# A table in place of the planner for the order of every engine, other buffer counts, and 256 more rows of x that come transposed from the host

## The chip, the cores and the metric

The kernel runs on one core of one Trainium2 chip. The metric is the device time of one execution in microseconds (us); shorter is better. A core has five engines with an instruction stream each: PE (TensorE, matrix products), DVE (VectorE), ACT (ScalarE), POOL (GpSimd) and SP (SyncE, which here only issues DMAs). Each runs its own stream strictly in order and waits for others on semaphores.

## What is computed

One layer over 2048 tokens of 1024 channels, batch 1, all in float32:

```
proj = rmsnorm(x) @ w_in                 # 1024 -> 3072: u, gate_ssm, q, k, v, gate_attn, 512 each
y_ssm = S5(u): complex diagonal scan over time (32 groups, 64 states), GELU, GLU
y_att = stick-breaking attention(q, k, v): 8 heads of 64, strictly causal, q and k RMS-normed
h = x + concat(y_ssm * silu(gate_ssm), y_att * silu(gate_attn)) @ w_out
out = h + sigmoid(rmsnorm(h) @ w_ple_gate) * (p @ w_ple_proj)
```

## The kernel before, in words

The 2048 tokens are 16 blocks of 128, taken two at a time (a pair T = 0 to 7 has 256 tokens). Each float32 operand of a large product is split into a high part, rounded to a narrower type that PE takes, and the rest: ACT writes the high part and DVE the low one (`split`, L511 to L514; for weights `load_w`, L473 to L496). A product is then three matmuls: high by high, high by low, low by high (`mm3`, L536, and `mm3x`, L702).

The work goes through four stages. First `phase_u` (L546): u for all eight pairs, 96 matmuls of 128x256 for each pair (8 chunks of the 1024 channels, 4 column tiles, 3 products). Meanwhile DVE works through `ssm_chain`, some hundreds of short operations that prepare the scan. Second, from L1204, the gate of the SSM half for every pair (`gate_unit`, L642) together with the eight batches of the scan (`ssm_pack`, `ssm_batch`) and the first attention projections. Third, from L1228, 40 steps of attention in four passes of two heads each, one pass 8 steps behind the other: `attn_proj` (L712) makes q, k, v and the gate of a block two blocks ahead, `attn_block` (L795) does one block of queries, and late steps carry the GLU (`glu_unit`) and sums of weights. Fourth, `phase_out` (L1038): the output projection and the gated embedding, each with a scheme of seven half-size products in place of eight.

**Where the rows of x come from.** The products need x transposed (channels on partitions), and scaled by its norm. For pair 0 (`load_plain`, L552) the host hands over the first 256 rows of x already transposed (`turned_x`, L1610). They are split as they are, without the norm; the norm of each token is worked out beside the products (`norms`, L573: squares on ACT, three adds on POOL, a sum by PE against ones, a power on POOL, and a product with a diagonal that spreads it into `e.row`), and multiplied in where the products leave PSUM: L633 for u, L656 for the gate, L735 and L748 for attention. For pairs 1 to 7 (`load_x`, L588) the plain rows are loaded by DMA (L593), squared and summed on ACT (L596), normed through DVE and POOL (L597, `rms_rstd`), scaled on ACT (L598), transposed by PE in 16 pieces of 64x64 for each block (L526), and split. Both forms then write the split block to DRAM (`hn_d`), from which later stages read it. The plain rows rest in XB = 4 buffers of one block each.

**PSUM.** u's four column tiles of a pair take one bank each: for pair 0 from the list w0, w1, o, acc, z0, z1, for later pairs from w0, w1, o, acc, in turn (L620). The transposes of `load_x` go through z0 and z1. So pair 1 takes the four banks that pair 0 filled.

**One block of attention** (L805 to L844) walks over up to four chunks of 512 keys, the newest first. For each chunk: products of q and k into `ps_z` (contraction over the 64 channels of a head, two heads abreast on the two halves of PE's rows), a sigmoid on ACT (L816), a running product on DVE (L821), 64x64 transposes on PE into `ps_wt`, and a copy with 1 - x on ACT into `ws` (L835). The products of `ws` with v into `ps_o` (L843; 64 output columns, two heads abreast on the two halves of PE's columns) are not made chunk by chunk but held until HOLD = 2 chunks have gathered or the block ends. A block with one or two chunks thus has one such burst, a block with three or four has two. `ws` rests in WSB = 5 buffers.

**The order.** The program is first written down in the order of the Python code. `arrange` (L1563) then gives every engine its order: `plan` works out for each instruction which others it needs and, by `duration` (L1295), an estimated length; `best_order` (L1530) runs a list scheduler forward and backward six times and keeps the order with the shortest estimated end. Two hints matter at the start: what is written inside `e.first()` ranks ahead of all else, and DMAs inside `e.later(k)` start no sooner than the instruction marked k (mark 0 is the load of weight chunk 7, L484). The order is fixed when the program is built; on the chip nothing is reordered.

The 16 KB at the start of each SBUF partition is scratch for the descriptors of DMAs that POOL issues: 8 writes of u (L638), the table of the scan, some constants, and the loads of the first pair of `phase_out`.

## Time and profile before

| what | before |
|---|---|
| median of 3 runs (lowest to highest) | 1474.67 us (1472.99 to 1477.0) |
| the profiled execution | 1474.24 us |
| its span, first to last instruction | 1472.5 us |
| mean granted clock of TensorE | 0.994 |
| busy: PE, weight loads beside it, DVE, ACT, POOL | 98%, 83%, 69%, 55%, 32% |
| instructions | 33586 |

The profile is of one execution, whose time is 1.7 us over its span (start and end lie around it) and 0.4 us under the median. In its lines an engine's name is followed by the line of the kernel, the operation, the tile written, an arrow and the tiles read. In a timeline the first two columns are the start and the length in us, and a bracket names the idle time before and what ended it. A matmul's length is the time until its result is out; matmuls overlap, so the pace is read from one start to the next. In the stage table (a window per row) each engine has its busy time and, in parentheses, its instructions.

### The profile page before, as it was taken

The page shows a single profiled execution, that of the slowest core. Times are in us where ns is not written, and L with a number is a line of the kernel's source. Part 1 is how long each engine was busy: PE and PEld are TensorE (multiplying, and loading weights), DVE is VectorE, ACT ScalarE, POOL GpSimd, SP SyncE. Part 2 cuts the span into 40 slices and gives each one's busy share as a digit, 9 for nine tenths or more (in the row PEclk, how much of TensorE's full clock was granted, in tenths as well). Part 3 has the DMA queues.
Part 4 walks back from the last instruction along what each step waited for, and adds up shares of the span by engine and source line. Part 5 has one row for each costly group of instructions (what it writes and reads, how often), then busy time and mean ns, then how long its engine had stood idle before and what let it go on. Part 6 is the DMA issues. An engine that isn't in the chain of part 4 may idle for free.

```text
span 1472.5 us, 33586 instructions
## 1 busy us (share of the span) xinstructions
PE 1436.7 (98%) x13068; PEld 1224.2 (83%) x13068; DVE 1009.0 (69%) x1817; ACT 810.4 (55%) x1765; POOL 474.8 (32%) x512
## 2 busy tenths in 40 slices
PE   6999999999999999999999999999999999999998
PEld 5999889988888888888888877777778888778786
DVE  8953977977567786678766775666778557754444
ACT  5654555565555766567655665555665345533432
POOL 3131363522221211221121124443334554534432
PEclk8999999999999999999999999999999999999999
DMA  8886845645333433334332455766568556523221
GB/s 289 288 287 205 250 143 186 206 143 168 128 130 125 144 112 114 114 130 140 121 126 102 142 146 171 226 218 178 155 201 280 176 171 200 166 65 101 93 72 58
DMA packets 179054, 238.21 MB, mean 162 GB/s; under 512 B 65760, under 2 KB 121296, under 8 KB 167760
## 3 DMA queue, kind: packets, MB, share of 16 engines
q1 hardware_dynamic: 176512, 227.49, 48.0%
q0 software_dynamic: 2384, 8.59, 2.0%
q8 instruction: 103, 1.69, 0.5%
q14 instruction: 55, 0.45, 0.1%
HBM read 166.94 MB, written 64.90 MB: 157 GB/s over the span
## 4 chain that ended last, share of the span: by engine, by line
PE 81%; DVE 7%; DMA 3%; ACT 3%; issue 3%; POOL 2%; SPq 1%; POOLq 0%; DVEq 0%; ACTq 0%
PE ps_q L745 21%; PE ps_o L843 7%; PE ps_z L812 6%; PE ps_wt L526 4%; PE ps_g L707 4%; PE ps_h L709 4%; PE ps_h L707 3%; PE ps_h L708 3%; PE ps_g L709 3%; PE ps_g L708 3%; DMA v<-qn 2%; PE ps_u L541 1%; PE ps_u L543 1%; PE ps_u L542 1%; PE ps_sg L541 1%
## 5 line engine op out<-in xcount | busy, mean ns | idle before, releaser
L821 DVE TENSOR_TENSOR_SCAN px<-px,ps_z 128x512 f32<-128x512 f32 (+3 forms) x320 | 339.9, 1086 | 85.9 <-ACT px L816 61.0
L745 PE MATMUL ps_q<-w_w,xt 64*128 64x512 f32 x2784 | 376.7, 399 | 1.3 <-DVE qn L65 0.7
L745 PEld LDWEIGHTS ps_q<-w_w,xt 64*128 64x128 f32 x2784 | 270.8, 185 | 39.7 <-DVE qn L65 2.2
L816 ACT ACTIVATE px<-ps_z 128x512 f32<-128x512 f32 (+3 forms) x320 | 159.2, 535 | 81.0 <-PE ps_z L812 79.8
L835 ACT ACTIVATE ws<-ps_wt 128x512 f32<-128x512 f32 (+3 forms) x320 | 160.7, 539 | 72.0 <-PE ps_wt L526 67.1
L812 PE MATMUL ps_z<-k,q 64*128 64x512 f32 (+3 forms) x960 | 137.7, 379 | 3.7 <-DVE px L821 1.8
L843 PE MATMUL ps_o<-ws,v 128*64 128x128 f32 x2176 | 134.9, 276 | 0.0
L843 PEld LDWEIGHTS ps_o<-ws,v 128*64 128x64 f32 x2176 | 117.3, 137 | 17.6 <-issue 14.7
L507 POOL TENSOR_TENSOR rs_qk<-rs_qk,mhalf 128x4 f32<-128x4 f32 x64 | 67.7, 1058 | 150.7 <-DVE rs_qk L72 148.1
L526 PEld LDWEIGHTS ps_wt<-ident,px 64*128 64x128 f32 x2176 | 95.5, 138 | 24.3 <-ACT ws L835 5.2
L812 PEld LDWEIGHTS ps_z<-k,q 64*128 64x128 f32 x960 | 87.9, 186 | 21.7 <-issue 5.4
L526 PE MATMUL ps_wt<-ident,px 64*128 64x64 f32 x2176 | 100.7, 224 | 2.0 <-ACT ws L835 1.8
L819 POOL TENSOR_SCALAR_AFFINE_SELECT px<-px 128x128 f32<-128x128 f32 x128 | 40.7, 328 | 164.2 <-ACT px L816 154.3
L756 POOL TENSOR_TENSOR v<-qn,v 128x128 f32<-128x128 f32 x64 | 32.2, 503 | 167.6 <-DMA v<-qn 153.9
L541 PE MATMUL ps_u<-xt,w_w 128*128 128x256 f32 x256 | 76.0, 298 | 7.5 <-ACT w_w L491 6.2
L65 DVE TENSOR_TENSOR yr<-sx,yr 128x512 fp32r<-128x512 f32 x64 | 50.6, 814 | 42.2 <-ACT yr L513 41.8
L543 PE MATMUL ps_u<-xt,w_w 128*128 128x256 f32 x256 | 74.5, 297 | 1.9 <-DVE w_w L76 1.8
L542 PE MATMUL ps_u<-xt,w_w 128*128 128x256 f32 x256 | 75.3, 295 | 0.5 <-DVE xt L65 0.5
L1032 POOL TENSOR_TENSOR sg<-sg,h 128x512 f32<-128x512 f32 x28 | 40.1, 1437 | 92.1 <-DVE sg L65 91.9
L513 ACT ACTIVATE yr<-sx 128x512 fp32r<-128x512 f32 x64 | 39.1, 627 | 53.7 <-POOL sx L912 22.6
L65 DVE TENSOR_TENSOR qn<-ps_q,part 128x512 f32<-128x512 f32 x54 | 36.8, 682 | 42.6 <-ACT part L751 39.0
L513 ACT ACTIVATE yr<-yq 128x512 fp32r<-128x512 f32 x48 | 30.2, 629 | 53.3 <-PE ps_h L709 24.5
(438 smaller groups left out, 3486.5 us busy)
## 6 DMA issues: line engine op xcount, KB each, us to landing
xt<-hn SPq DMA_DIRECT2D x58, 1024.0 KB
hn<-xt SPq DMA_DIRECT2D x16, 1024.0 KB
h<-h SPq DMA_DIRECT2D x64, 256.0 KB
wst<-in_w_in_dram SPq DMA_DIRECT2D x48, 256.0 KB
xg<-hn SPq DMA_DIRECT2D x12, 1024.0 KB
out_dram<-sg SPq DMA_DIRECT2D x31, 256.0 KB
x<-in_x_dram SPq DMA_DIRECT2D x14, 512.0 KB
h<-in_x_dram SPq DMA_DIRECT2D x28, 256.0 KB
```

What stands on the lines that cost most here:

```text
L526: e.nc.tensor.transpose(ps[h][:, 64 * k:64 * k + 64], v[r], e.ident[r, r])
L541: mm(out, wh, xh, start=first, stop=False)
L542: mm(out, wh, xl, start=False, stop=False)
L543: mm(out, wl, xh, start=False, stop=last)
L707: mm(out, xh, wh, start=first, stop=False, skip_group_check=more)
L709: mm(out, xl, wh, start=False, stop=last, skip_group_check=more)
L745: nc.tensor.matmul(o, xt[r, a, c], A.w[c][r, b], start=c + s == 0, stop=c == NC8 - 1 and s == 2)
L812: nc.tensor.matmul(z[:, :n], q[half[h], a], A.k[ch][half[h], b, :n], start=s == 0, stop=s == 2)
L816: nc.scalar.activation(px[:, :n], z[:, :n], AF.Sigmoid, scale=-(HD ** -0.5))
L821: nc.vector.tensor_tensor_scan(rv, rv, z[:, :n][:, ::-1], initial=1.0 if carry[h] is None else carry[h], op0=ALU.mult, op1=ALU.bypass)
L835: nc.scalar.activation(dst, ps, AF.Copy, bias=1.0, scale=-1.0)
L843: nc.tensor.matmul(po[half[h], :P], A.v[sb][:, h], w[:, h, b], start=sb == i, stop=sb == 0)
```

## The change

The planner (`footprint`, `duration`, `plan`, `list_schedule`, `best_order`: some 280 lines) goes. In its place stands a table: a string that unpacks to one list of positions for each engine, from which `arrange` takes the instructions of each engine one by one. The order is again fixed when the program is built; which instructions the table moves cannot be read from the string.

```diff
-XB, ..., PXB, WSB, ... = 4, ..., 8, 5, ...
+XB, ..., PXB, WSB, ... = 6, ..., 8, 8, ...
-HOLD = 2
+HOLD = 4
+RAW = 2
+UB = ("z0", "z1", "w0", "w1"), ("o", "acc", "w0", "w1"), ("o", "acc", "w0", "w1")
...
             for hf in range(2):
                 x = plain[2 * T + hf]
-                nc.sync.dma_start(x[:, cs], e.xt[2 * T + hf, :, cs])
+                if T == 0 or c % 4 == 0:
+                    cd = cs if T == 0 else slice(c, c + 4)
+                    nc.sync.dma_start(x[:, cd], e.xt[2 * T + hf, :, cd])
                 split(e, xt[:, hf, 0, cs], xt[:, hf, 1, cs], x[:, cs])
...
         xts[0], w = load_plain(0)
+        with e.later(0):
+            xts[1], _ = load_plain(1)
         norms(0)
         norms(1)
-        with e.later(0):
-            xts[1] = load_x(1)
+    norms(2)
+    norms(3)
...
-        ps = [e.bank("ps_u", "w0", "w1", "o", "acc", *(("z0", "z1") if T < 1 else ()))[:, :256] for _ in range(4)]
+        ps = [e.bank("ps_u", *UB[min(T, 2)])[:, :256] for _ in range(4)]
...
-            if T < 1:
+            if T < RAW:
                 vt(nc, out, o, e.row[T].rearrange("p (c j) -> p j c", j=L), ALU.mult)
...
-        if T < 1:
+        if T < RAW:
             og = pool.tile([P, 256], F32, tag="sg", name="og", bufs=2)
...
-        if i < 2:
+        if i < 2 * RAW:
             nc.scalar.activation(flat, pq, AF.Copy, scale=e.rs[i])
...
-    warm = const("warm", [P, 24])[:, :1]
+    warm = const("warm", [P, 8])[:, :1]
...
-    e.rs = [const(f"rs{i}", [P, 1]) for i in range(2)]
+    e.rs = [const(f"rs{i}", [P, 1]) for i in range(2 * RAW)]
...
-    e.row = [gx.tile([P, 256], F32, tag=f"row{T}", name=f"row{T}") for T in range(1)]
+    e.row = [gx.tile([P, 256], F32, tag=f"row{T}", name=f"row{T}") for T in range(RAW)]
...
+def written_order(ops):
+    import base64, zlib
+    code = iter(zlib.decompress(base64.b85decode(_ORDER)))
+    for e in _ENGINES:
+        left = [i for i in ops if type(i).__name__ != "BassTilePoolBoundary" and str(i.engine).split(".")[-1] == e]
+        line = []
+        while left:
+            at, shift, c = 0, 0, 128
+            while c & 128:
+                c = next(code)
+                at |= (c & 127) << shift
+                shift += 7
+            line.append(left.pop(at))
+        yield line
 def arrange(tc, pools, rows):
-    ops, pre, *rest = plan(tc, pools)
-    _, order, _ = best_order(ops, pre, *rest, rows)
     info = mybir.DependencyInfo(mybir.DependencyClass.NoSync, mybir.DependencyReason.DATA)
-    for line in order.values():
+    for line in written_order(list(tc.nc.cur_bb.bb.instructions)):
...
-    nc = _bacc.Bacc("TRN2", target_bir_lowering=False, num_devices=1)
+    nc = _bacc.Bacc("TRN2", target_bir_lowering=False, num_devices=1, dynamic_dma_scratch_size=4096)
...
-            turned_x = _np.ascontiguousarray(a[0, :2 * P].reshape(2, P, NC8, P).transpose(0, 3, 2, 1))
+            turned_x = _np.ascontiguousarray(a[0, :2 * RAW * P].reshape(2 * RAW, P, NC8, P).transpose(0, 3, 2, 1))
```

So pair 1 of x now comes as pair 0 did: transposed, in four DMAs of half a block each, split without a norm, and multiplied by the norm at the exits of u, gate and projections. Pair 0 takes the banks z0, z1, w0, w1 and pair 1 o, acc, w0, w1. Two more blocks of x can be loaded ahead (XB 4 to 6). A block of attention holds all its chunks (HOLD 2 to 4) and makes one burst of products with v; three more buffers of 4 KB a partition hold `ws` (WSB 5 to 8), in the 12 KB that the smaller DMA scratch leaves free.

327 lines of the change are left out of this document (77 added, 250 removed).

## Prediction

> **What bounds the kernel now.** First the page, for the busiest engine.
>
> ```profile
> PE 1436.7 (98%) x13068; PEld 1224.2 (83%) x13068; DVE 1009.0 (69%) x1817; ACT 810.4 (55%) x1765; POOL 474.8 (32%) x512
> ```
>
> PE is busy for all but 1472.5 - 1436.7 = 35.8 us of the span. So the change can gain in three ways only: fill PE's idle time, remove PE work, or make PE's work run at a better pace. Next, where the idle time lies, in a table of stages. Its columns are the stretch, its length, the busy time of PE, PEld, DVE, ACT and POOL (instructions in parentheses), the clock, the DMA share and GB/s.
>
> ```profile
> 0.00:26.00 26.00, 17.18 (x98) 15.96 (x98) 21.21 (x119) 14.16 (x24) 10.68 (x22) 0.93 0.83 287
> 26.00:41.00 15.00, 10.26 (x74) 9.05 (x73) 14.98 (x79) 10.15 (x17) 4.54 (x7) 0.66 0.75 277
> 41.00:129.20 88.20, 87.37 (x837) 84.69 (x837) 55.08 (x162) 47.80 (x88) 20.42 (x19) 1.00 0.81 272
> 129.20:315.00 185.80, 182.18 (x1465) 171.48 (x1463) 151.40 (x263) 103.29 (x236) 74.94 (x43) 1.00 0.61 188
> 315.00:1100.00 785.00, 774.86 (x8953) 647.55 (x8954) 545.58 (x894) 474.52 (x1104) 201.75 (x306) 1.00 0.47 147
> 1100.00:1250.00 150.00, 149.98 (x662) 123.01 (x660) 102.28 (x146) 70.90 (x149) 77.35 (x55) 1.00 0.64 206
> 1250.00:1472.50 222.50, 214.89 (x989) 172.44 (x988) 118.45 (x160) 89.57 (x151) 85.11 (x61) 1.00 0.29 94
> ```
>
> 8.8 us of the idle time lie before 26 us, 4.7 in the next 15 us, where the clock is 0.66 as well, and 10.1 in the 785 us of attention. From 41 us on PE is 99% busy, so whatever PE does earlier before 41 us moves the rest of the program up by as much, as long as the other engines follow. Now the timeline of PE at the place the change works on, the step from pair 0 to pair 1 and on to pair 2.
>
> ```profile
> 25.77 0.28 PE L543 MATMUL ps_u<-xt,w_w 128*128 128x256 f32 x1
> 26.85 0.49 PE L585 MATMUL ps_row<-dg,ones 128*128 128x128 f32 x2 [0.80 <-DVE dg L70]
> 31.43 1.11 PE L526 MATMUL ps_x<-ident,x 64*128 64x64 f32 x16 [1.40 <-ACT x L598]
> 33.72 0.58 PE L541 MATMUL ps_u<-xt,w_w 128*128 128x256 f32 x1 [1.17 <-ACT xt L513]
> 35.41 0.42 PE L541 MATMUL ps_u<-xt,w_w 128*128 128x256 f32 x1
> 35.62 0.41 PE L542 MATMUL ps_u<-xt,w_w 128*128 128x256 f32 x1
> 39.46 0.32 PE L542 MATMUL ps_u<-xt,w_w 128*128 128x256 f32 x1
> 49.67 0.28 PE L541 MATMUL ps_u<-xt,w_w 128*128 128x256 f32 x1
> 50.03 0.28 PE L541 MATMUL ps_u<-xt,w_w 128*128 128x256 f32 x1
> 129.06 0.60 PE L340 MATMUL ps_pack<-ident,bn 128*128 128x128 f32 x4
> ```
>
> Pair 0 ends at 26.05 us. Pair 1 starts at 33.72, held in turn by the scaling of x, the transposes and the split. Its first products start 0.21 us apart (35.41, 35.62), up to 39.46; later ones 0.12 (49.67 to 50.03 holds three). Pair 2 starts at 50.03, and the six pairs 2 to 7 end at 129.06: 79.03 / 6 = 13.2 us a pair, with the transposes of the next pair inside.
>
> **The change part by part: pair 1.** Transposed x needs no norm ahead of the products, so Square, power, scaling and 32 transposes leave the path of pair 1; eight splits of 128x256 stay. What the other engines do for it:
>
> ```profile
> 13.22 0.78 ACT L513 ACTIVATE xt<-x 128x256 fp32r<-128x256 f32 x2
> 19.48 1.06 ACT L575 ACTIVATE x<-x 128x1024 f32<-128x1024 f32 x1 [3.19 <-DVE xt L65]
> 20.44 1.32 ACT L491 ACTIVATE w_w<-wst,gmix 128x512 fp32r<-128x512 f32 x2
> 27.12 1.15 ACT L598 ACTIVATE x<-x,rs_x 128x1024 f32<-128x1024 f32 x1 [2.18 <-POOL rs_x L507]
> 29.06 1.09 ACT L513 ACTIVATE xt<-ps_x 128x512 fp32r<-128x512 f32 x2 [0.63 <-PE ps_x L526]
> 20.62 4.71 POOL L577 TENSOR_TENSOR x<-x 128x512 f32<-128x512 f32 x4 [14.25 <-ACT x L575]
> 24.59 5.38 SPq L593 DMA_DIRECT2D x<-in_x_dram  x3
> 31.01 0.57 DVE L65 TENSOR_TENSOR uq<-ps_u,row 128x256 f32<-128x256 f32 x1
> L65 DVE TENSOR_TENSOR og<-ps_sg,row 128x256 f32<-128x256 f32 x4 | 1.7, 415 | 0.1
> ```
>
> ACT does not gain work: for a block of pair 1 it did a Square (about 1.06), the scaling 1.15 and two splits 1.09, together 3.3 us; now four splits at 0.39 and a Square 1.06, together 2.6. The two splits that close pair 0's weights run at 20.44 to 21.8, behind a Square that had waited 3.19 us; pair 1's splits (8 x 0.39 = 3.1 us) can follow at once and its first product need not wait past about 26. The banks agree: pair 1 now starts in o and acc, which pair 0 does not use, while before it waited for pair 0's exit, which starts at 31.01, after the norm. The two extra norms load POOL (3 adds and a power each, a few us a block by the row at 20.62) in a stretch where it works 4.5 of 15 us. Pair 1's exit must wait for its norm, but its first bank is wanted again only by pair 2.
>
> So pair 1 starts at 26.05 and takes a pair's 13.2 us, plus about 1.5 for the row products of four norms that stand in PE's order (two of their waits were 0.80 and less): pair 2 starts at 40.8 instead of 50.0. **Gain 9.2 us.** A part of it, (39.46 - 33.72) / 0.213 = 27 products at most at 0.213 instead of 0.12, is 2.5 us of clock, because the idle stretch before pair 1 is gone. The Trainium skill (TensorE: Matmul & The Clock Gate, Part 1: The HAM clock gate) says that the throttle is lifted after some 3.4 us of sustained work. The trace shows 5.7 us at the slow pace here; by the page's figure the clock's part would be 1.5 us and the whole gain, as an estimate, 8.2.
>
> Ends: if the order also lets pair 0's last weights go ahead of the Square, up to its 3.19 us more, 12.4. If pair 2's rows come too late (their loads started at 24.59, as buffers came free; with six buffers they need not wait), PE waits there for as long as it waited for pair 1, 33.72 - 26.05 = 7.7, and 9.2 shrinks to 1.5. I take 9.2, since ACT is idle for 16.7 us of the first 41 and DVE's chain of short operations, which fills its time to 41 us, can wait: DVE is idle for 33 us of the stage after. DMAs: as many bytes as before, four of 256 KB in place of two of 512; XB only lets them start earlier.
>
> Costs at the exits lie on DVE: four products of 0.57 us in place of ACT's copies, and four of 0.415 for the gate (its row is the last above, for pair 0), in stages where DVE is idle for 33 and 34 us. Zero on the path; with that cover gone, 4 x 0.57 + 4 x 0.415 = 3.9. The projections keep their instructions and only take a scale.
>
> **HOLD and WSB.** By L837 a pass of 16 blocks has 8 x 1 + 8 x 2 = 24 bursts of products with v before and 16 after: 96 and 64 over four passes. In PE's timeline many stand back to back; I count 73 stretches of them, from the first to the last row here. What a burst costs beside its own work is read in the same timeline.
>
> ```profile
> 322.85 0.44 PE L843 MATMUL ps_o<-ws,v 128*64 128x128 f32 x4
> 323.22 0.72 PE L745 MATMUL ps_q<-w_w,xg 64*128 64x512 f32 x4
> ...
> 562.55 0.97 PE L745 MATMUL ps_q<-w_w,xt 64*128 64x512 f32 x6
> 563.45 1.97 PE L843 MATMUL ps_o<-ws,v 128*64 128x128 f32 x32
> 565.35 0.96 PE L812 MATMUL ps_z<-k,q 64*128 64x512 f32 x6
> ...
> 566.30 2.33 PE L745 MATMUL ps_q<-w_w,xt 64*128 64x512 f32 x18
> 568.46 0.46 PE L812 MATMUL ps_z<-k,q 64*128 64x128 f32 x6
> ...
> 1097.20 1.97 PE L843 MATMUL ps_o<-ws,v 128*64 128x128 f32 x32
> ```
>
> Six q products take (568.46 - 566.30) / 3 = 0.72 us, but 0.90 (562.55 to 563.45) with a burst behind them: 0.18 to enter. Bursts take 0.37 us for 4 products and 1.90 for 32, so 0.055 each and 0.15 fixed, to leave. A burst thus costs 0.33 us beyond its products. Of 73 stretches, 64 x 73 / 96 = 49 would be left; since longer bursts may merge less often I take 20 fewer: 20 x 0.33 = **6.6 us**. Ends: 9 fewer (none of the 64 merging) at 0.15, if the neighbours pay the 0.18 to each other, are 1.4, and 32 at 0.33 are 10.6. The products themselves stay. WSB adds no instruction; it lets ACT's copies run two whole blocks ahead.
>
> **The table.** It is a fixed order as the planner's was, so by itself it adds no wait. Of the 10.1 us that PE idles in attention and the 3.6 in the stage before, another order can take some. I put this at 3 us, a third of the 10.1, and its ends at 0 and 12, nearly all of it; an order that waits more is a rival below.
>
> **Sum** against the profiled execution's own time: 1474.24 - 9.2 - 6.6 - 3 = **1455.4 us**; that execution lies 0.4 under the median of 1474.67, so no shift is made. Low end: 1474.24 - 12.4 - 10.6 - 12 = 1439.2. High end of the same case: 1474.24 - 1.5 - 1.4 = 1471.3. A change under 0.3% (4.4 us) could hardly be told from none.
>
> **Rivals.** (1) *The bursts do not pay*: those that go were adjacent anyway, or PE pays the same 0.33 between other kinds. Then 1474.24 - 9.2 - 3 = 1462. For it: 96 bursts in 73 stretches means that 23 are merged already. Against it: the 64 that are left can merge too. Chance 0.15.
>
> (2) *Held bursts make PE wait, slower than before.* With HOLD 4 the products of the old chunks no longer fill the time of the newest chunk's chain, from sigmoid to running product to copy:
>
> ```profile
> L816 ACT ACTIVATE px<-ps_z 128x512 f32<-128x512 f32 x224 | 125.6, 599 | 68.8 <-PE ps_z L812 68.0
> L821 DVE TENSOR_TENSOR_SCAN px<-px,ps_z 128x512 f32<-128x512 f32 x224 | 276.9, 1261 | 70.0 <-ACT px L816 61.0 <-POOL px L819 7.9
> L835 ACT ACTIVATE ws<-ps_wt 128x512 f32<-128x512 f32 x224 | 127.1, 603 | 56.6 <-PE ps_wt L526 51.7 <-PE ps_o L843 4.5
> ```
>
> That is 0.60 + 1.26 + 0.60 = 2.5 us. 32 blocks have three or four chunks. While projections of several passes run, PE has other products; in the last ten steps of attention, with one pass left, ten such blocks remain. If the chain lies open once in each, that is 25 us, and with the gains at the start and in the bursts 1474.24 + 25 - 9.2 - 6.6 = 1483. It is slower than before from 15.8 / 2.5, some 7 open chains, on. Against it: PE's 10.1 us of idle time in attention are four such chains in all, and the GLU's products stand in those steps. Chance 0.10.
>
> (3) *POOL waits for its smaller scratch.* The four writes of u:
>
> ```profile
> 69.53 1.24 POOL L638 DMA_DIRECT2D u<-uq  x1
> u<-uq POOLq DMA_DIRECT2D x8, 512.0 KB, 7.8
> ```
>
> Each lands 7.8 us after its issue. If a quarter of the scratch holds only one at a time, three wait 7.8 - 1.2 = 6.6 each, 20 us, with the power of the next rows' norm queued behind them on POOL, and the scaling, the transposes and PE behind that. Six buffers of x cover one pair, 13.2 us; PE loses about 7 twice at most: 1462 to 1469. The Trainium skill (DMA: Bandwidth & Descriptors, SWDGE vs HWDGE vs iDMA) says that the descriptors of such DMAs are written to rings in a carve-out of SBUF; no run here shows how full it is. Chance 0.07, and 0.03 that it, with a late pair 2, leaves no gain.
>
> The forecast has the rest, 0.65. Faster: 0.63 of it, 0.13 of rival 1 and 0.04 of rival 3, 0.80 in all. The same: 0.02 from each of the first two, whose high ends lie within the bound, and 0.06 from rival 3, so 0.10. Slower: rival 2, 0.10. The range, 1439 to 1474, takes in the ends of the sum and rivals 1 and 3, and leaves out rival 2 and little else.
>
> **What the profile after would show.** Right: the first product of pair 2 near 41 us, the clock near 1 from 26 to 41, no transposes before pair 1, row products at four blocks; stretches of products with v near 50, up to 128 products long; PE's idle time near 25 us. Wrong: pair 2 waiting for ACT or POOL; PE idle in attention above 15 us, put down to the copies at L835; POOL's issues of u longer than 1.2 us.

## The result and the profile after

The changed kernel takes 1516.43 us (median of 4 runs, 1513.09 to 1523.13) against 1474.95 for the kernel before, measured beside it: a ratio of 1.0287 [1.0249, 1.0325]. It is slower by some 41 us; the prediction said 1455.4, in a range of 1439 to 1474. The profiled execution took 1517.1 us with a span of 1515.3, and its mean granted clock was 0.983 (before 0.994).

The busy times on the page after, in the form of the prediction's first line:

```profile
PE 1441.8 (95%) x13044; PEld 1230.5 (81%) x13044; DVE 1028.9 (68%) x1831; ACT 806.1 (53%) x1763; POOL 467.6 (31%) x518
```

PE did the same work in nearly the same busy time (1441.8 against 1436.7). It is idle for 1515.3 - 1441.8 = 73.5 us in place of 35.8, so about 38 of the 43 us that the span grew are new waiting. The stage table shows where; its columns are as in the prediction, and the cut at 129.2 is the end of u before, the one at 162.7 its end now.

```profile
0.00:26.00 26.00, 9.31 (x38) 8.44 (x39) 20.14 (x111) 10.03 (x17) 6.14 (x17) 1.00 0.71 245
26.00:41.00 15.00, 14.46 (x115) 14.30 (x114) 14.62 (x48) 11.31 (x23) 8.68 (x12) 1.00 0.64 242
41.00:129.20 88.20, 65.40 (x545) 61.62 (x546) 64.51 (x201) 38.71 (x68) 17.79 (x23) 0.85 0.63 221
129.20:162.70 33.50, 33.50 (x308) 32.90 (x307) 8.30 (x13) 10.64 (x23) 2.37 (x2) 1.00 0.56 184
162.70:353.00 190.30, 182.66 (x1446) 172.02 (x1444) 142.75 (x263) 102.75 (x231) 72.80 (x44) 0.98 0.60 183
353.00:1136.00 783.00, 765.75 (x8870) 640.99 (x8869) 548.44 (x888) 468.94 (x1098) 195.05 (x303) 0.99 0.46 146
```

One thing came as forecast: from 26 to 41 us PE is busy for 14.46 us at a clock of 1.00, where before it was 10.26 at 0.66. But it lost 8 us ahead of that (9.31 busy in the first 26 us against 17.18), and from 41 to 129.2 it idles for 22.8 us where before it idled for 0.8, at a clock of 0.85. PE's timeline at the breaks (a bracket holds the idle time before and what ended it; the third row is the first product of pair 2, the fourth is in pair 5's transposes):

```profile
11.92 1.22 PE L544 MATMUL ps_u<-xt,w_w 128*128 128x256 f32 x4 [3.08 <-DVE xt L67]
21.27 1.23 PE L545 MATMUL ps_u<-xt,w_w 128*128 128x256 f32 x4 [5.56 <-DVE w_w L78]
...
55.20 0.39 PE L543 MATMUL ps_u<-xt,w_w 128*128 128x256 f32 x1 [0.32 <-DVE uq L67]
...
116.32 1.11 PE L528 MATMUL ps_x<-ident,x 64*128 64x64 f32 x15 [10.11 <-DVE xt L67]
```

Pair 2 starts at 55.2 us (forecast 40.8, before 50.0), and near 116 us PE stands still for 10.1 us at a stretch.

The stages of all kernels of this study, read from PE's timelines, in us from the span's start. "Pair n" is the first of its 96 products of u, "u done" the last product of u, "attention" the first product of q or score of that stage, "scores done" the last score, "end" the last product.

| kernel | pair 1 | pair 2 | pair 4 | u done | attention | scores done | end | time |
|---|---|---|---|---|---|---|---|---|
| before | 33.7 | 50.0 | 77.4 | 129.2 | 315.5 | 1090.1 | 1467.9 | 1474.95 |
| after | 34.0 | 55.2 | 95.3 | 162.7 | 353.1 | 1125.8 | 1510.7 | 1516.43 |
| before, 4 KB scratch | 33.9 | 49.4 | 76.9 | 138.1 | 324.7 | 1102.6 | 1480.4 | 1486.87 |
| before, 8 KB scratch | 33.8 | 50.0 | 77.3 | 129.1 | 315.4 | 1093.2 | 1471.0 | 1477.36 |
| after, 8 KB scratch | 33.4 | 55.9 | 96.0 | 151.0 | 336.7 | 1115.8 | 1495.2 | 1497.05 |
| after, splits of pair 0 ahead | 33.3 | 55.7 | 95.8 | 163.1 | 349.8 | 1124.1 | 1505.5 | 1512.33 |
| after, 8 KB, start repaired | 28.1 | 57.6 | 97.7 | 153.0 | 338.9 | 1113.1 | 1494.2 | 1497.19 |
| after, 8 KB, rows 8 ahead | 33.2 | 55.8 | 97.1 | 151.5 | 335.9 | 1108.2 | 1487.8 | 1498.26 |
| after, 8 KB, rows 25 ahead | 32.8 | 55.3 | 101.6 | 156.9 | 342.8 | 1118.0 | 1497.9 | 1506.60 |
| after, planner | 26.0 | 44.4 | 74.4 | 141.6 | 338.6 | 1130.6 | 1515.1 | 1520.31 |
| after, planner, 8 KB | 26.1 | 47.2 | 77.0 | 132.9 | 329.8 | 1117.4 | 1502.5 | 1507.58 |
| the same, HOLD 2 | 26.0 | 46.0 | 77.3 | 133.3 | 326.9 | 1112.5 | 1490.1 | 1496.38 |
| before, HOLD 4 | 33.8 | 50.7 | 78.1 | 129.9 | 316.1 | 1089.2 | 1473.6 | 1478.72 |
| before, turned pair, 8 KB | 26.1 | 45.8 | 74.4 | 132.4 | 324.5 | 1103.8 | 1481.6 | 1488.43 |
| before, turned pair, 16 KB | 26.0 | 50.7 | 81.1 | 138.4 | 320.4 | 1106.9 | 1484.6 | 1489.42 |
| the 8 KB one, exits without norm | 25.7 | 43.6 | 75.2 | 132.4 | 321.8 | 1105.9 | 1483.9 | 1488.02 |
| the 8 KB one, another bank | 26.0 | 46.2 | 75.9 | 128.7 | 322.1 | 1104.5 | 1482.2 | 1490.06 |
| before, short chain | 34.1 | 50.3 | 76.7 | 128.7 | 318.4 | 1095.8 | 1473.7 | 1477.89 |
| turned pair 8 KB, short chain | 25.3 | 47.7 | 76.4 | 136.4 | 327.3 | 1108.9 | 1486.7 | 1492.99 |

The times are medians, the other columns are one profiled execution each. Of the kernel after's loss at the end (1510.7 - 1467.9 = 42.8 us), 33.5 stand at the end of u, 4.1 more at the start of attention; attention takes back 1.9, and the last stage loses 7.1. The last two belong together: in the kernel after some 75 products of attention more than before stand behind the last score, so part of the 7.1 is work moved over that cut.

### The profile page after: what moved, and what is told of

It reads as the page before. It is cut to its first block, busy times and chain, and to the rows that moved or that the text cites. A ratio compares the mean times of both kernels' runs of the same rounds, so it can differ in the third digit from the quotient of the medians.

```text
span 1515.3 us, 33475 instructions
## 1 busy us (share of the span) xinstructions
PE 1441.8 (95%) x13044; PEld 1230.5 (81%) x13044; DVE 1028.9 (68%) x1831; ACT 806.1 (53%) x1763; POOL 467.6 (31%) x518
## 4 chain that ended last, share of the span: by engine, by line
PE 78%; DVE 7%; DMA 5%; issue 5%; ACT 3%; POOL 1%; SPq 1%; POOLq 0%; DVEq 0%; ACTq 0%
PE ps_q L751 21%; PE ps_o L849 6%; PE ps_z L818 6%; PE ps_wt L528 4%; PE ps_g L713 3%; PE ps_g L714 3%; PE ps_g L715 3%; PE ps_h L715 3%; PE ps_h L713 3%; PE ps_h L714 3%; DMA wst<-in_ssm_w_glu_dram 2%; PE ps_sg L543 1%; PE ps_sg L545 1%; PE ps_sg L544 1%; PE ps_v L543 1%
## 5 line engine op out<-in xcount | busy, mean ns | idle before, releaser
L751 PE MATMUL ps_q<-w_w,xt 64*128 64x512 f32 x2784 | 372.7, 400 | 0.3
L751 PEld LDWEIGHTS ps_q<-w_w,xt 64*128 64x128 f32 x2784 | 270.0, 188 | 40.7 <-DVE qn L78 0.8
L841 ACT ACTIVATE ws<-ps_wt 128x512 f32<-128x512 f32 (+3 forms) x320 | 156.5, 540 | 76.1 <-PE ps_wt L528 75.3
L849 PE MATMUL ps_o<-ws,v 128*64 128x128 f32 x2176 | 132.9, 276 | 0.8 <-DVE yat L67 0.8
L849 PEld LDWEIGHTS ps_o<-ws,v 128*64 128x64 f32 x2176 | 117.5, 137 | 12.7 <-issue 8.5
L528 PEld LDWEIGHTS ps_wt<-ident,px 64*128 64x128 f32 x2176 | 91.5, 139 | 35.6 <-ACT ws L841 16.2
L818 PEld LDWEIGHTS ps_z<-k,q 64*128 64x128 f32 x960 | 91.5, 188 | 16.3 <-DVE px L827 4.5
L825 POOL TENSOR_SCALAR_AFFINE_SELECT px<-px 128x128 f32<-128x128 f32 x128 | 39.6, 319 | 192.1 <-ACT px L822 190.7
L543 PE MATMUL ps_u<-xt,w_w 128*128 128x256 f32 x256 | 69.1, 308 | 9.3 <-ACT xt L515 8.7
L544 PE MATMUL ps_u<-xt,w_w 128*128 128x256 f32 x256 | 69.2, 304 | 5.7 <-DVE xt L67 5.7
L545 PE MATMUL ps_u<-xt,w_w 128*128 128x256 f32 x256 | 68.7, 303 | 5.6 <-DVE w_w L78 5.6
L1038 POOL TENSOR_TENSOR sg<-sg,h 128x512 f32<-128x512 f32 x28 | 40.8, 1462 | 94.4 <-DVE sg L67 87.4
L67 DVE TENSOR_TENSOR yr<-sx,yr 128x512 fp32r<-128x512 f32 x64 | 58.0, 923 | 10.9 <-ACT yr L515 10.3
L78 DVE SCALAR_TENSOR_TENSOR w_w<-wst,gmix,w_w 128x512 fp32r<-128x512 f32 x48 | 38.1, 803 | 34.4 <-ACT w_w L493 34.3
L543 PEld LDWEIGHTS ps_u<-xt,w_w 128*128 128x128 f32 x256 | 50.2, 212 | 10.6 <-ACT xt L515 8.9
```

What stands on the lines that cost most here:

```text
L528: e.nc.tensor.transpose(ps[h][:, 64 * k:64 * k + 64], v[r], e.ident[r, r])
L543: mm(out, wh, xh, start=first, stop=False)
L544: mm(out, wh, xl, start=False, stop=False)
L751: nc.tensor.matmul(o, xt[r, a, c], A.w[c][r, b], start=c + s == 0, stop=c == NC8 - 1 and s == 2)
L818: nc.tensor.matmul(z[:, :n], q[half[h], a], A.k[ch][half[h], b, :n], start=s == 0, stop=s == 2)
L841: nc.scalar.activation(dst, ps, AF.Copy, bias=1.0, scale=-1.0)
```

## The experiments

### The scratch for POOL's descriptors

*Theory*: the first stage stalls because a quarter of the scratch lets only one write of u be in flight, and the norms of later rows wait behind on POOL. *Rival*: that stall is harmless, and the loss comes from the table's order. POOL's timeline in the kernel after, the four writes of u and the power of a row's norm behind them; then ACT's next scaling of x:

```profile
86.66 1.21 POOL L644 DMA_DIRECT2D u<-uq  x1
97.92 1.17 POOL L644 DMA_DIRECT2D u<-uq  x1 [10.05 <-issue]
106.25 1.15 POOL L644 DMA_DIRECT2D u<-uq  x1 [7.16 <-issue]
111.35 1.16 POOL L644 DMA_DIRECT2D u<-uq  x1 [3.94 <-issue]
112.53 0.56 POOL L509 TENSOR_TENSOR rs_x<-rs_x,mhalf 128x1 f32<-128x1 f32 x1
```

```profile
113.12 1.15 ACT L602 ACTIVATE x<-x,rs_x 128x1024 f32<-128x1024 f32 x1 [16.75 <-POOL rs_x L509]
```

"issue" means that POOL waited for nothing that the profile shows. It stands before three writes, 21.2 us in all. What it waited for can be read from the landings: the first write landed at 97.45 us and the second was issued at 97.92; the second landed at 105.95, the third was issued at 106.25. The norm comes out at 113.1, ACT had waited 16.75 us for it, and PE's 10.11 us above follow. They follow through the orders of ACT and VectorE and not through the rows themselves: the scaling is of pair 6, while the transposes that PE waits to make are of pair 5. In ACT's order the high part of a weight stands behind the scaling (114.18), VectorE's low part of that weight waits for it (114.92), and behind that stands the split of pair 5 (115.58) that frees the bank. To see the scratch alone, it was changed in the kernel before:

```diff
-    nc = _bacc.Bacc("TRN2", target_bir_lowering=False, num_devices=1)
+    nc = _bacc.Bacc("TRN2", target_bir_lowering=False, num_devices=1, dynamic_dma_scratch_size=4096)
```

> The kernel before with the DMA scratch of 4096 bytes and nothing else, its planner's order unchanged. In the changed kernel POOL issues its first write of u at 86.66 us, then sits idle 10.05, 7.16 and 3.94 us ahead of the other three, put down to issue. Scratch theory: those waits are for room in the smaller scratch, so they come here too: the four writes, issued at 69.5 to 79.5 us before, spread over some 25 to 30 us, the powers of the norms queue behind them on POOL, and PE idles 8 to 15 us in pairs 4 to 6: 1483 to 1490 us. Table theory (all of the loss comes from the order in the table, the waits on POOL only follow from a late DVE): no wait between the writes, 1475 us as before.

Measured: 1486.87 us, 1.0082 [1.0067, 1.0097]. In its POOL timeline the same pattern stands, with no other edit:

```profile
77.03 1.20 POOL L638 DMA_DIRECT2D u<-uq  x1 [2.25 <-ACT uq L635]
85.33 1.15 POOL L638 DMA_DIRECT2D u<-uq  x1 [7.10 <-ACT xt L513]
95.44 1.16 POOL L638 DMA_DIRECT2D u<-uq  x1 [8.96 <-issue]
96.62 0.56 POOL L507 TENSOR_TENSOR rs_x<-rs_x,mhalf 128x1 f32<-128x1 f32 x1
```

The row that waited 7.10 us is put down to a split on ACT, which the write has nothing to do with: with 8 KB, below, the same write goes out at 76.98. It is the same wait under another name. Up to pair 4 this kernel is level with the one before, and u is done 8.9 us later. Then 8 KB in place of 4, in both programs (in the kernel after, one buffer of `ws` makes the room: WSB 8 to 7):

> The kernel before with 8192 bytes of scratch instead of 16384, nothing else. Theory A (room for about three writes of u at a time is enough): a wait of POOL under 4 us on one write of each group of four, no late pair, 1474 to 1478. Theory B (any write that must wait delays the norm behind it): half of what 4096 bytes cost, 1480 to 1483. What it shows is also the share of the scratch in the three runs that have 8192 bytes.

> The changed kernel with a scratch of 8192 bytes and 7 buffers of ws in place of 8, the table as it is. Scratch theory: three writes of u can be under way at once, the waits of 10.05 and 7.16 us on POOL go, PE's wait of 10.1 us at 106 us goes, and the time falls by 10 to 15 us to 1502 to 1506; the late start of pair 1 at 34 us and of pair 4 at 95 stays. Table theory: POOL's waits stay as they are and so does the time, 1516 us.

Measured: 1477.36 us in the kernel before (1.0014 [1.0003, 1.0024]), and 1497.05 in the kernel after (1.0141 [1.0118, 1.0164] of before). POOL in these two, the kernel before first:

```profile
75.19 1.19 POOL L638 DMA_DIRECT2D u<-uq  x1
76.98 1.15 POOL L638 DMA_DIRECT2D u<-uq  x1 [0.60 <-ACT uq L635]
78.66 1.16 POOL L638 DMA_DIRECT2D u<-uq  x1 [0.52 <-ACT w_w L491]
```

```profile
87.41 3.50 POOL L644 DMA_DIRECT2D u<-uq  x3
97.99 1.16 POOL L644 DMA_DIRECT2D u<-uq  x1 [7.08 <-ACT xt L515]
```

With 8 KB three writes go out in a row (3.50 us for three), and only a fourth that comes at once has to wait: it is issued at 97.99, the first had landed at 97.53. So 4 KB cost 11.8 us in the order of before (1486.87 against 1475.11 beside it), and 8 KB only 2.1; in the order of after, 4 KB cost 19.4 us more than 8. The theory holds for about half of the loss. The rest, some 22 us, is not the scratch's; in the kernel after with 8 KB most of it stands at the end of u (151.0 - 129.2 = 21.8, of 27.3 at the profiled end).

### The table

The planner was put back into the changed program, once with 4 KB of scratch and once with 8 KB and WSB 7:

```diff
-    for line in written_order(list(tc.nc.cur_bb.bb.instructions)):
+    ops, pre, *rest = plan(tc, pools)
+    _, order, _ = best_order(ops, pre, *rest, rows)
+    for line in order.values():
```

> The changed kernel with the planner of before in place of the table, the scratch still 4096 bytes. Table theory: pair 0 ends near 26 us, pair 2 starts near 41, and the forecast's 1455 us come out, or 1475 at most. Scratch theory alone: the start improves, but POOL's waits cost PE 8 to 15 us in pairs 4 to 6 as before: 1465 to 1475 us. If HOLD 4 itself costs time, the stage of attention is longer than the 785 us of before.

> The changed kernel with the planner in place of the table, a scratch of 8192 bytes and 7 buffers of ws. With 4096 bytes the planner's version took 1520.3 us: pair 2 began at 44.4 us, 5.7 earlier than before, but pairs 3 to 5 took 17.8, 24.5 and 19.0 us each with POOL waiting between the writes of u. Scratch theory: those 20 us go and the time is about 1500; what is then left over 1475 lies in the later stages, where that version took 14 us more in the gate stage and 17 us more in attention than before. If the later losses are consequences of the scratch too (a late u, PE's clock falling after each wait), 1470 to 1480.

Measured: 1520.31 us (1.0313 [1.0293, 1.0332]), where 1455 to 1475 was expected, and 1507.58 (1.0216 [1.0198, 1.0233]). At 4 KB the intervals of table and planner overlap; at 8 KB the table is 10.5 us the better. It loses at the start and wins it back: with 8 KB u is done at 151.0 with the table and at 132.9 with the planner, but from there to the end the table takes 1344.2 us, the planner 1369.6. So the table is not what makes the change slow as a whole, though its first stage is 18 us worse than what the planner finds for the same program.

Why is that stage so long? The trace of the kernel after offered an answer: in VectorE's order the chain's short operations stand ahead of the weights' low parts. Between these two rows of its timeline lie 8.9 us, filled with them but for two splits of x, and PE's 5.56 us at 21.27 wait for the second:

```profile
10.79 0.75 DVE L78 SCALAR_TENSOR_TENSOR w_w<-wst,gmix,w_w 128x512 fp32r<-128x512 f32 x1
...
20.47 0.74 DVE L78 SCALAR_TENSOR_TENSOR w_w<-wst,gmix,w_w 128x512 fp32r<-128x512 f32 x1
```

Three repairs of that order were tried, each an edit of the table's list for VectorE as it is unpacked: the 16 splits of pair 0 and its weights go as far ahead as in the kernel before (4 KB); those of the first two pairs, with ACT's first two squares moved behind the eighth weight (8 KB); and, later, row operations ahead of up to 8 or 25 chain operations from pair 2's first split to pair 3's last (8 KB).

```diff
-    for line in written_order(list(tc.nc.cur_bb.bb.instructions)):
+    for e, line in zip(_ENGINES, written_order(list(tc.nc.cur_bb.bb.instructions))):
+        line = earlier(line) if e == "DVE" else line
```

> The changed kernel with one repair of the table: on DVE the 16 splits of pair 0's x and weights stand behind as few short operations of the scan's preparation as before (for the sixth split 37 and not 88). Table theory: pair 0 ends near 27 us in place of 34.2, everything after it comes 6 to 8 us earlier, 1508 to 1511 us; more, if the late transposes of pair 4 at 85.7 us are a consequence of DVE's late start. Scratch theory alone: the gain at the start is lost again in POOL's waits, 1514 to 1517 us.

> The changed kernel with 8192 bytes of scratch and 7 buffers of ws (1497.1 us), and the start of the table repaired on two engines: on DVE the splits of the first two pairs go ahead of the short operations, on ACT the squares of pair 0's norm go behind the last weights. If the table's start is what is left, pair 0 ends near 24 us instead of 33.6 and the time falls 8 to 12 us, to 1485 to 1489, or by up to 20 if the late transposes of pair 4 at 86 us go too. If DVE's work as a whole holds the first stage up, pair 7 ends at 150 us as before and the time stays at 1497.

> The changed kernel with 8 KB of scratch and WSB 7, and one more edit of VectorE's order: between pair 2's first split and pair 3's last, the row operations (splits of x and weights, norms, exits) go ahead of up to 8 of the scan's short operations, whose own order stays. Theory A (the queue's order: rows wait behind the chain): pair 4 starts 2 to 5 us before 96.0, and the time is 1492 to 1496 against 1497.0. Theory B (VectorE is simply full up to 96 us, and what is put back must be done before pair 4's splits all the same): pair 4 within 1.5 us of 96, 1496 to 1499.

> The same with row operations ahead of up to 25 of the scan's short operations. Theory A (order): pair 4 starts 5 to 12 us before 96.0, the first stage ends before 145, the time is 1486 to 1493. Theory B (full): pair 3 earlier, pair 4 within 2 us of 96, since the 25 operations put back and the first packs of the scan then stand ahead of pair 4's splits; 1495 to 1500.

Measured: 1512.33 us (1.0254 [1.0233, 1.0274], against 1516.43), 1497.19 (1.0149 [1.0129, 1.0169], against 1497.05), 1498.26 (1.0162 [1.0137, 1.0188]) and 1506.60 (1.0227 [1.0205, 1.0249]). The first gains some 4 us (its interval overlaps that of the kernel after), but not as expected: pair 1 starts at 33.3, where 27 was forecast. The next two gain nothing, and the last loses 9.6 us. In the second, pair 1 does start 5 us earlier, at 28.1, but takes until 55. In the last two pair 4 starts later than without the edit. The stage tables of two kernels from 26 to 96 us suggest what was missed; first the kernel after with 8 KB, then the kernel before with the turned pair and 8 KB, which the planner ordered:

```profile
26.00:60.00 34.00, 30.46 (x247) 28.54 (x247) 32.77 (x100) 19.11 (x37) 13.76 (x19) 0.90 0.79 291
60.00:96.00 36.00, 26.00 (x227) 24.35 (x225) 34.59 (x133) 18.20 (x32) 7.55 (x9) 0.87 0.49 175
```

```profile
26.00:60.00 34.00, 32.13 (x297) 30.59 (x296) 32.68 (x150) 22.27 (x38) 12.19 (x19) 0.95 0.89 324
60.00:96.00 36.00, 32.00 (x298) 30.58 (x296) 27.75 (x88) 20.20 (x37) 8.83 (x10) 1.00 0.78 260
```

In the table's order VectorE is busy for 34.6 of the 36 us from 60 to 96. What is taken out of one place of its queue comes back in the next, ahead of pair 4's splits. The planner's order has 150 of VectorE's instructions done between 26 and 60 us where the table has 100, and so has room afterwards. So a full queue, not one misplaced operation, fits all four runs. It is an argument and not shown: neither the table without the chain nor a table with another first stage was run.

### HOLD

*Theory of the prediction*: fewer bursts of products with v save 6.6 us. *Rival*: the held products leave the newest chunk's chain uncovered.

```diff
-HOLD = 2
+HOLD = 4
```

> The kernel before with HOLD 4 and nothing else (planner, 5 buffers of ws, scratch of 16384 bytes). By the forecast's second term there are about 20 fewer bursts of products with v at 0.33 us each: 1468 us. Rival (held bursts make PE wait): a block with four chunks holds four of the five buffers, the next block's copies wait for the burst, and attention takes 10 to 20 us longer: 1485 to 1495 us.

Measured: 1478.72 us, 1.0021 [1.0012, 1.0030]: a loss of some 3 us, 5.7 by the profiled end. PE's timeline counts exactly 64 stretches of products with v, one for each block, of 4 to 64 products, where the kernel before has 73. The kernel after has 64 too. So 9 stretches went, not 20: of the 64 that are left none merges. Attention itself took 1089.2 - 316.1 = 773.1 us against 774.6: the gain is 1.5 us, the prediction's low end. It is lost where attention hands over to the output projection. PE's timeline there, first the kernel before, then with HOLD 4:

```profile
1090.58 0.71 PE L526 MATMUL ps_wt<-ident,px 64*128 64x64 f32 x16 [0.48 <-ACT ws L835]
1091.23 1.97 PE L843 MATMUL ps_o<-ws,v 128*64 128x128 f32 x32
1093.12 0.50 PE L707 MATMUL ps_h<-w_w,yr 128*128 128x512 f32 x1
```

```profile
1088.27 0.97 PE L812 MATMUL ps_z<-k,q 64*128 64x512 f32 x6
1089.07 0.66 PE L526 MATMUL ps_wt<-ident,px 64*128 64x64 f32 x16
1092.48 0.80 PE L707 MATMUL ps_h<-w_w,yr 128*128 128x512 f32 x1 [2.75 <-ACT yr L513]
```

Before, 32 products with v (1.97 us) fill PE between the last transposes and the output projection; with HOLD 4 they are still held, and PE stands for 2.75 us and again for 0.96 at 1129. The first wait fits the rival's open chain (2.5 us by the prediction): sigmoid, running product and copies run from 1089.3 to 1092.4, and PE has nothing from 1089.7 on. What ends the wait by the profile is the split of `yr`, which stands in ACT's order behind these copies. The wait costs more than its own length: from 1089.2 to 1104.0 us the granted clock is 0.77, where before, from 1090.1 to 1105.0, it was 1.00. From the last score to the end the kernel takes 384.4 us in place of 377.8; PE idles 3.7 us more, and the same products keep it busy 2.9 us longer. The same edit was priced in the changed program under the planner (8 KB, WSB 7), by putting HOLD back to 2:

> The changed program with the planner, 8192 bytes of scratch, WSB 7 and HOLD back at 2. Against the same with HOLD 4 (1507.6) it prices the held bursts in this program. Theory A (holding costs, since the products with v no longer fill the chain of the newest chunk): attention falls from 788 us to near 776 and the time to 1492 to 1498, about that of the turned pair alone (1488.4) and a little. Theory B (holding is neutral, as it was in the kernel before, +3.8 us; the long attention comes from another order that the planner falls into): 1503 to 1510.

Measured: 1496.38 us (1.0141 [1.0124, 1.0158]) against 1507.58 with HOLD 4. The time fell as the first theory said, but most of it at another place: attention took 785.6 us against 787.6, while from the last score to the end it was 377.6 us in place of 385.1. There too PE waited for `ws` (2.2 us) and `yr` at the hand-over with HOLD 4. The 11 us are little more than two orders of the planner can differ by (8 us, below).

### The turned pair

Now the part that the prediction valued most, alone in the kernel before: RAW = 2, the banks `UB`, the halved loads, two more norms, and the exits and scales that belong to them; planner, HOLD 2 and WSB 5 stay. Six buffers of x only fit with 8 KB of scratch, so it was run with XB 6 and 8 KB, and with XB 4 and the full 16 KB.

```diff
+RAW = 2
+UB = ("z0", "z1", "w0", "w1"), ("o", "acc", "w0", "w1"), ("o", "acc", "w0", "w1")
...
+        with e.later(0):
+            xts[1], _ = load_plain(1)
         norms(0)
         norms(1)
-        with e.later(0):
-            xts[1] = load_x(1)
+    norms(2)
+    norms(3)
```

> The kernel before with only the start of the change: pair 1 of x transposed by the host, its norm at the exits, the new banks and six buffers of x (for which the scratch is 8192 bytes); planner, HOLD 2 and 5 buffers of ws as before. By the forecast's first term pair 2 starts near 41 us and the time falls 9 us, 1466. Rival: the halved scratch and DVE's extra products at the exits give it back by the end of the first stage, 1473 to 1478.

> The kernel before with pair 1 of x turned by the host and nothing else: the planner, HOLD 2, WSB 5, four row buffers and the full 16 KB of scratch. It differs from the run with 8 KB of scratch and six row buffers (1488.4) in these two alone. Theory A (the turned pair itself costs, since the second norm's and exit's operations fall into the stretch before 90 us in which VectorE has nothing to spare): the same pattern, 1482 to 1490, pair 2 near 46 us, VectorE idle for under 3 of the 30 us from 60 to 90, and the end of the first stage after 129. Theory B (the loss of that run is the halved scratch): the forecast's own gain shows, pair 2 before 47 and the first stage done before 127; 1466 to 1476.

Measured: 1488.43 us (1.0088 [1.0069, 1.0107]) and 1489.42 (1.0090 [1.0073, 1.0107]). The loss is there with either scratch and number of buffers: the turned pair itself costs 13 to 14 us in the planner's order. (The four buffers do matter early on: PE waits 3.7 us for scaled rows, and pair 2 starts at 50.7, not near 46.) Pair 1 does start at 26, as forecast. PE's timeline in the first of the two, and VectorE's exit of pair 0, show what happens in it:

```profile
32.42 0.28 PE L545 MATMUL ps_u<-xt,w_w 128*128 128x256 f32 x1
33.43 0.46 PE L589 MATMUL ps_row<-dg,ones 128*128 128x128 f32 x2 [0.74 <-DVE rs_x L74]
34.88 0.38 PE L583 MATMUL ps_row<-ones,x 128*128 128x1 f32 x2 [0.98 <-DVE uq L67]
35.19 1.07 PE L528 MATMUL ps_x<-ident,x 64*128 64x64 f32 x16
36.23 0.55 PE L543 MATMUL ps_u<-xt,w_w 128*128 128x256 f32 x1
...
45.76 0.39 PE L543 MATMUL ps_u<-xt,w_w 128*128 128x256 f32 x1
```

```profile
34.24 0.58 DVE L67 TENSOR_TENSOR uq<-ps_u,row 128x256 f32<-128x256 f32 x1
```

The products of pair 1 break off at 32.42 and go on at 36.23, after the first exits of pair 0 (34.24), which are products with the norm's row; ACT has the row ready at 34.21. Pair 1's third and fourth column tile lie in w0 and w1, which pair 0 still holds. The kernel after has the same break, after 48 products of pair 1, and there the third tile's first product (the last row) waits for the exit by name:

```profile
39.87 0.28 PE L545 MATMUL ps_u<-xt,w_w 128*128 128x256 f32 x1
...
42.72 0.25 PE L528 MATMUL ps_x<-ident,x 64*128 64x64 f32 x1 [1.34 <-DVE uq L67]
...
43.99 0.39 PE L543 MATMUL ps_u<-xt,w_w 128*128 128x256 f32 x1 [0.16 <-DVE uq L67]
```

In the run alone pair 2 starts at 45.8, a gain of 4.2 us; but u is done at 132.4, later than before. And that is the smaller part: of the 13.7 us at the profiled end, 3.2 stand there, 5.8 come in the stage of the gate (192.1 us against 186.3; PE idles 9.8 against 4.1) and 4.7 in attention.

Two explanations were open: VectorE's fullness, or the banks that the norm at the exit holds. For the first, the powers and tables of the chain were left out and their results filled with constants by POOL (96 operations and 12 to 13 us of VectorE, where some 110 and about 25 were expected), in the kernel before and in the one with the turned pair; the scan's results are then not the reference's.

```diff
-    while n < L:
-        ...
-        cmul(e, sm, pr[:, n + 1:2 * n + 1], pi[:, n + 1:2 * n + 1], pr[:, 1:n + 1], pi[:, 1:n + 1], *bc, [n, G])
+    nc.gpsimd.memset(pr[:, 2:], 0.5)
+    nc.gpsimd.memset(pi[:, 2:], 0.25)
```

> The kernel before, with the powers and the tables of the scan's chain left out: some 110 short operations of VectorE (about 25 us) go, and the tables are filled with constants, so the scan's results are not those of the reference. It is the partner of the next run. Theory A (VectorE bounds the first stage only with the turned pair; in the kernel before the early wait of PE is for the norm of pair 1): pair 2 moves by 2 us at most from 50.0, the first stage still ends at 126 to 129, and the time is 1466 to 1474. Theory B (VectorE holds the kernel before as well): pair 2 before 47, the first stage done before 125.

> The kernel before with the turned pair 1 (8 KB of scratch, six row buffers), with the same part of the scan's chain left out. Theory A (the chain on VectorE took the room that the forecast counted on): with it gone the forecast's gain appears: pair 2 near 41, the first stage done at 119 to 124 instead of 132.4, and the run 4 to 10 us below its partner without the turned pair. Theory B (rows, banks or clock hold it): pair 2 at 45 or later, the first stage done at 128 to 133, and the run no faster than its partner.

Measured: 1477.89 us (1.0002 [0.9988, 1.0015]) and 1492.99 (1.0101 [1.0079, 1.0122]). For what happens after 60 us the theory that VectorE has no room falls: the stage table of the second shows room for it there,

```profile
26.00:60.00 34.00, 29.84 (x254) 28.47 (x255) 31.36 (x121) 19.71 (x35) 15.25 (x23) 0.90 0.93 330
60.00:75.00 15.00, 14.09 (x135) 13.49 (x135) 10.59 (x19) 11.14 (x20) 7.03 (x6) 1.00 0.72 229
75.00:90.00 15.00, 14.57 (x142) 14.09 (x140) 7.24 (x10) 6.41 (x11) 6.09 (x6) 1.00 0.97 321
```

17.8 of 30 us busy, and still u is done at 136.4 and the kernel is 15 us behind its partner. Up to 60 us VectorE stays about as full as it was (31.4 us of 34, against 32.7), so about pair 1, and the start of pair 2 at 47.7, this run decides nothing. For the second explanation, the exits of u were made plain copies on ACT that wait for no norm (u of the first 512 tokens stays unscaled), and in another kernel pair 1 got the bank tr as its third:

```diff
-            if T < RAW:
-                vt(nc, out, o, e.row[T].rearrange("p (c j) -> p j c", j=L), ALU.mult)
-            else:
-                nc.scalar.activation(out, o, AF.Copy)
+            nc.scalar.activation(out, o, AF.Copy)
```

```diff
-UB = ("z0", "z1", "w0", "w1"), ("o", "acc", "w0", "w1"), ("o", "acc", "w0", "w1")
+UB = ("z0", "z1", "w0", "w1"), ("o", "acc", "tr", "w0"), ("o", "acc", "w0", "w1")
...
-        ps = e.bank("ps_row", "tr", "ssm")
+        ps = e.bank("ps_row", "ssm")
```

> The kernel before with the turned pair 1 (8 KB of scratch, six row buffers), but the exits of u for pairs 0 and 1 are plain copies on ACT that do not wait for the norm: u of the first 512 tokens is left unscaled. Theory A (the norm at the exit holds PSUM banks that PE needs next): PE's standstill near 33 to 36 us goes, pair 1 takes 13 to 15 us in place of 19.7, pair 2 starts at 40 to 42 and the first stage ends at 120 to 126 instead of 132.4. Theory B (the order of the row products or the rows' arrival holds PE anyway): pair 2 at 44 or later, stage end 130 or later. The stages behind it may gain or lose some us by the planner's other order.

> The kernel before with the turned pair 1 (8 KB of scratch, six row buffers), the row products kept to one bank, and pair 1's column tiles in o, acc, tr and w0 instead of o, acc, w0 and w1: 72 products of pair 1 in place of 48 can run before one of pair 0's banks must be free. The outputs are those of the reference. Theory A (the norm at the exit holds the banks): 24 products, about 3 us, move ahead of the standstill, pair 2 starts 2 to 4 us earlier than 45.8. Theory B (something else holds PE): pair 2 within 1 us of 45.8. In the time, 1480 to 1490 either way, since the gate stage has its own loss.

Measured: 1488.02 us (1.0067 [1.0042, 1.0092]) and 1490.06 (1.0086 [1.0064, 1.0107]). Without the norm at the exit PE runs through pair 1 without a stop, from 25.7 to 40.7: 15.0 us, what the prediction had (13.2 and 1.5). With the norm it takes 19.1 us from its first product to its last (26.1 to 45.2). So the norm at the exit does hold the banks, and that costs pair 1 some 4 us. The other bank confirms it: PE breaks off pair 1 after its 72nd product, at 35.6, and no longer after the 48th, at 32.4. The end of the PE timeline without the norm shows the next wait:

```profile
40.56 0.38 PE L589 MATMUL ps_row<-dg,ones 128*128 128x128 f32 x2
42.01 0.25 PE L528 MATMUL ps_x<-ident,x 64*128 64x64 f32 x1 [1.07 <-DVE xt L67]
42.60 1.08 PE L528 MATMUL ps_x<-ident,x 64*128 64x64 f32 x15 [0.35 <-DVE pr_nr L72]
43.62 0.58 PE L543 MATMUL ps_u<-xt,w_w 128*128 128x256 f32 x1
```

Pair 2 starts at 43.6, a lead of 6.4 us over before, and at pair 4 the lead is 2.2 us (75.2 against 77.4); u is done at 132.4, 3.2 us late. With the other bank pair 2 did not come earlier (46.2), against the expectation of 2 to 4 us, but u was done at 128.7, and then 7.1 us went in the stage behind. In every kernel with the turned pair under the planner the lead is spent by the end of u but for half a microsecond in one. With 8 KB and the full chain (five kernels), it goes at two places: pair 3 takes 16.1 to 18.8 us, where it took 14.2, and pair 5 takes 15.5 to 19.8, where it took 13.4. In the first kernel of this section pair 5 starts at 88.6 with a lead of 2.0 us and takes 19.8:

```profile
97.05 0.27 PE L528 MATMUL ps_x<-ident,x 64*128 64x64 f32 x1 [1.69 <-DVE xt L67]
```

The split that PE waits for came late though VectorE had stood idle for 8.09 us: ACT's half of it (95.68) stands in ACT's order behind an exit of u (95.40), which needs a product of pair 5. PE idles 2.9 us in pair 5, and the clock is 0.83 in it (1.00 before). So there it is the planner's order and not a full engine, and the slow clock costs about as much as the waits. Why the stages behind u take longer, and whether another order would keep the lead, is not settled; each program gets an order of its own. How far such orders lie apart is seen in two programs that differ in two buffers of `ws` only: 1488.43 with WSB 5, 1496.38 with WSB 7 (the changed program with HOLD 2). A single planner-made run therefore prices an edit to no better than some 8 us; that all six such kernels with HOLD 2 lie 0.7 to 1.4% above before, and none below, is the firmer finding.

One way through the runs puts the parts side by side, by medians: 1475.0 us before, 1488.4 with the turned pair (8 KB, six row buffers), 1496.4 with two more buffers of `ws`, 1507.6 with HOLD 4, 1520.3 with 4 KB and WSB 8, and 1516.4 with the table in place of the planner. The steps are 13.4, 8.0, 11.2, 12.7 and -3.9 us; in the table's order the step from 8 to 4 KB is 19.4. A step of some 8 us may be no more than another order.

No kernel of the study was faster than the one before.

## Why the prediction was wrong, point by point

**The frame: the step that failed first.** "From 41 us on PE is 99% busy, so whatever PE does earlier before 41 us moves the rest of the program up by as much, as long as the other engines follow." They don't follow. Even with plain exits, pair 2 was 6.4 us ahead and the kernel 0.7% slower. Of the eight kernels in which the planner ordered a turned pair, seven had a lead at pair 2 (2.3 to 6.4 us over the kernel before), and one had half a microsecond of it left at the end of u. A stage in which PE is 99% busy is not one in which the rows of x come with time to spare: in pair 5 above, waits of 2.9 us and a slow clock took the lead.

**Pair 1, 9.2 us: wrong.** The step that failed is "The banks agree: pair 1 now starts in o and acc, which pair 0 does not use". It starts there; its third and fourth tile lie in w0 and w1, which pair 0 fills as well, so the exit of pair 0, with its norm, stood on the path of pair 1 (the break from 32.42 to 36.23, and the slow pace after it). The prediction asked only when pair 1's own first bank is wanted again. By the run with plain exits that costs pair 1 some 4 us. The `UB` lines were quoted beside the prediction and say so. Right were the start at 26 us under the planner, and the 14.7 us that pair 1 takes once the exit is free (15.0). "DVE's chain of short operations, which fills its time to 41 us, can wait" did not hold in the table's order, which ran the chain first; in the planner's programs it stays open, since the short chain left VectorE full up to 60 us. In the kernel after pair 1 started at 34.0, and pair 2 at 55.2.

**The bursts, 6.6 us: a mis-sized term.** 20 fewer were assumed, 9 it is: merging by chance, counted at 23 in the kernel before, does not survive when each block makes one burst. 9 x 0.15 = 1.4 was the low end given, and attention alone gained 1.5; rival 1, that the bursts do not pay, was nearer than the term. The term's sign in the whole is the other one: some 3 us lost in the kernel before and 11 in the changed program under the planner, mostly behind attention, at the hand-over to the output projection, a place that the prediction didn't look at.

**The table, 3 us: right in sign at last, wrong in shape.** With 8 KB of scratch it is 10.5 us better than the planner for the same program. The statement that a fixed order "by itself adds no wait" was the error: its first stage is 18 us worse.

**Rival 2** had the mechanism, but at one place instead of ten: 2.75 us, against 2.5 forecast for an open chain, and not in attention but at its end; that the two lengths agree is in part luck, since a split in ACT's order ended the wait. **Rival 3** was right, and the largest single term: three waits and "20 us" on POOL were forecast, 21.2 measured. With 4 KB in the kernel before, norm, scaling, transposes and PE follow as described (PE waits 7.48 us for the scaling); in the kernel after the delay passes through the orders of ACT and VectorE. Its price was near as well: PE would lose 7 to 14 us, and the runs show 11.8 in the kernel before, 12.7 in the changed one with the planner and 19.4 with the table (there with one buffer of `ws` changed too). What failed is its weight. It was set against gains that it would only reduce, with 0.10 for all its outcomes. The sentence "with the power of the next rows' norm queued behind them on POOL" names the whole damage; a row that shows 7.8 us to landing and an edit that takes three quarters of the descriptors' room should have been read as the likeliest case.

**The signs named in advance**: pair 2 near 41 (55.2), clock near 1 from 26 to 41 (1.00), stretches near 50 and up to 128 products long (64, and at most 64 long), PE idle near 25 us (73.5). Of these all but the clock spoke against the forecast. Of the signs of "wrong", the writes of u that waited came as named. Pair 2 was late, though its last wait is put down to VectorE's exit and not to ACT or POOL. PE's idle time in attention is 14.8 us up to the last score and 17.3 in the row of the table above, against a mark of 15; 9.0 of it are put down to the copies (1.8 before). The longest of these waits, 4.48 us at 903, is not the open chain: ACT had stood 5.21 us for a weight of the GLU that comes ahead of the copies in its order.

## What to carry to other kernels

When a multiplication moves from the loading of an operand to the exit of its product, list which PSUM banks the next products need and ask when that factor is ready: the exit, not the load, is then on the path. Before taking memory from the descriptors of GpSimd's DMAs, add up how many of its transfers are in flight together and what stands behind the next issue on that engine. A stage at 99% for one engine says nothing of how far ahead its suppliers run; a head start at its beginning is worth what the slowest supplier can keep of it.

## What the runs showed of the hardware

A DMA issue on POOL takes about 1.2 us for a write of u and, when there is no room for its descriptors, stands still until an earlier transfer has landed (97.45 and 97.92 above): with 4 KB of scratch the writes of u (512 KB each) went one at a time, with 8 KB three in a row. The trace gives these waits as "issue" or under the name of an engine that the write does not need. The Trainium skill (DMA: Bandwidth & Descriptors, Terms) says that such descriptors are written to rings in SBUF; how many transfers fit is what these runs add.

VectorE's short operations became long while POOL added two tiles from SBUF. POOL's and VectorE's timelines of the kernel before with the turned pair (8 KB):

```profile
30.68 3.21 POOL L581 TENSOR_TENSOR x<-x 128x512 f32<-128x512 f32 x3
```

```profile
29.73 0.28 DVE L72 TENSOR_SCALAR dg<-ident,rs 128x128 f32<-128x128 f32 x1
...
30.68 1.34 DVE L67 TENSOR_TENSOR pr_cs<-sc_z,sc_mc 128x32 f32<-128x32 f32 x1
31.95 1.34 DVE L72 TENSOR_SCALAR dg<-ident,rs 128x128 f32<-128x128 f32 x1
```

The same product with the diagonal takes 0.28 us at 29.73, where no addition runs, and 1.34 beside the additions. The Trainium skill (SBUF — State Buffer, SBUF: two separate sides) describes one pair of ports that VectorE and GpSimd share and that one of them holds for a whole instruction; the rows agree. The prediction counted the additions of the two new norms as POOL's load alone; here they also took some 1.1 us from each of two operations of VectorE. The second of these makes the diagonal of the row that the exit of pair 0 waits for, so by an estimate from these rows (2 x 1.1) the new norms themselves made that exit some 2 us later.
